# Time mixing with seven slots per head pair in place of eight, and a chain of 35 steps

## The chip, the core and the metric

The kernel runs on one core of a Trainium2 chip. The metric is the time of one execution in microseconds (us), measured on the device; lower is better. One program computes the whole trunk, and the change touches one stage of it.

## What is computed

A trunk of two layers over 256 tokens of width 2048, in float32, with 32 heads of 64. Every sub-layer has an RMS norm, a shift and scale and a gate that come from a condition vector `c` (adaLN). Layer A mixes over time with the recurrence below and ends in an MLP; layer B is chunked attention over a shared K/V, and another MLP. The change concerns the time mixing of layer A, cut here to what matters:

```python
xr, xw, xk, xv, xa, xg = [h + xx * mu[j] for j in range(6)]
r = xr @ w_r
k = xk @ w_k
v = xv @ w_v
...
def step(S, inp):
    r_t, w_t, k_t, v_t, kk_t, a_t = inp
    sa = jnp.einsum('bhvk,bhk->bhv', S, -kk_t)
    S = (S * w_t[:, :, None, :] + sa[..., None] * (kk_t * a_t)[:, :, None, :]
         + v_t[..., None] * k_t[:, :, None, :])
    y = jnp.einsum('bhvk,bhk->bhv', S, r_t)
    return S, y
...
y = ((y - mean) * lax.rsqrt(var + GN_EPS) * ln_w + ln_b)
y = y + jnp.sum(r_h * k_h * r_k, axis=-1, keepdims=True) * v_h
y = y * g
return y @ w_o
```

## The kernel before

Activations lie transposed, features on partitions. Weights come from HBM as float32 in tiles of 128 x 1024 (0.5 MB, tile `raw`, six buffers) and are split into a high and a low half: ScalarE casts `wH` (L378), VectorE subtracts to `wL` (L381), three buffers each. A projection (`proj2`) multiplies each 128-row block with `wH` against both halves of the activations (L412, 512 columns) and with `wL` against the high half (L413, 256 columns). Condition vectors of the later parts (adaLN) are summed on VectorE while other work runs: one `ada_step` reads one `raw` tile and adds it to `acc` (L454).

The 32 heads are 16 pairs, two heads on the 128 partitions, and time is cut into four chunks of 64 tokens. The class `Pair` writes a pair's whole work as a generator of 36 steps:

- **early**, steps 0 to 7: decay, normalized key, the factors `kr`, `bh`, `kh` (tiles `s`, L163 to L175, on VectorE), transposes of v.
- **invert**, steps 8 to 19. The recurrence within a chunk becomes the inverse of a triangular 64 x 64 matrix. Step 8 makes the products `gr` with `bh` and from them the masked `ar` (L212) and the pieces `da`, `co`; step 9 completes the start value `u`. Then five levels of two steps: the first transposes `u` to `tt` on VectorE (L239) and multiplies with the level's mask (`iv<-tt,al`, L111), ScalarE copies the product to `xs`; the second multiplies `iv<-u,xs` (L111), and VectorE adds it to `u` (L254). So levels 1 to 5 are steps 10/11, 12/13, 14/15, 16/17 and 18/19. Step 13 also makes the products `gr` with `kh` (L105) and the masked `mk` (L263). The last level works on the off-diagonal corner in a bank `ms`, and VectorE copies it into `uf` (L258).
- **late**, steps 20 to 35: for each of four chunks three steps with 64-wide products into the bank `lt` (L280 to L302), where the chunk's state goes on in `zs` (L307), then the group norm, the bonus and the gate. `py`, the result before the norm, lies in `lt`. ScalarE squares it in step 32, TensorE sums over heads in step 33, ScalarE takes the reciprocal root in step 34 and VectorE multiplies `py` with `ln_w` and that (L320), and step 35 makes the gate's product (L324) and applies it (L326).

`layer_a` lays the pairs out in slots. `SLOTS` is 8: pair j starts in slot 8(j+1), so that in a full slot four or five pairs are under way, each at another step: steps k, k+8, k+16, k+24 and so on share a slot (k is called the phase). In a slot the pairs' steps are issued first, those of the inversion first of all, then the late ones, then the early ones, each with the larger step first. They are pinned in this order on TensorE by `issue_after`; behind them come two of the 16 dense steps in which the next pair's k and r are projected (`proj_steps`, two row blocks each). The sum of the two halves of such a projection is taken on VectorE (L861, tiles `k` and `r`). On the other engines a scheduler fixes the order of instructions ahead of time, each engine running its own list strictly in order. From slot 16 on, three of four slots also take an adaLN step, 111 in all. After the last projection, from slot 128, the dense steps are 44 steps of the output projection `w_o` (`out_steps`), spread over the remaining 36 slots while the last pairs finish.

PSUM, the memory that matmuls write, has eight banks: `gr` and `iv` have one each, `ms`, `lt` and `pj` more. A bank is free again when its last reader is done.

Of the kernel before, what the change touches and what calls it, by code (L numbers as in the profile page):

```python
# [77 lines left out]
class Pair:  # L78

    EARLY, INVERT, LATE = 8, 12, 16  # L80
# [107 lines left out]
    def corner(self, l):  # L188
        t = self.b.psm() if l == 5 else self.b.pp.tile([P, 512], F32, tag="iv", bufs=1, name="iv")
        return t.rearrange("p (c t) -> p c t", t=H)[:, 0:4, :]  # L190

    def invert(self):
# [18 lines left out]
        ar = self.ar = s("ar", 3)  # L211
        nc.vector.tensor_tensor(out=ch(ar), in0=pg[:, :, C:P], in1=ui[:, :, C:P], op=ALU.mult)  # L212
# [24 lines left out]
        for l in range(1, 6):  # L237
# [13 lines left out]
            pi = self.corner(l)  # L251
            if l < 5:
                self.tiles(pi, xs, u, [(i, i) for i in range(4)])
                nc.vector.tensor_tensor(out=u, in0=u, in1=pi, op=ALU.add)  # L254
            else:
                self.tiles(pi, xs, u, up)
                for K in QS[::2]:
                    nc.vector.tensor_copy(uf[K, :, H:C], pi[K])  # L258
# [7 lines left out]
    def late(self):  # L266
# [45 lines left out]
        sq = self.square(py)  # L312
        yield
        var = b.psm()[:, :T]
        self.head_sums(var, sq)
        yield
        rg = s("sl", 1)
        nc.scalar.activation(rg, var, AF.Ln, scale=1.0 / C, bias=b.col(C_GN))
        nc.scalar.activation(rg, rg, AF.Exp, scale=-0.5)
        nc.vector.scalar_tensor_tensor(out=rg, in0=py, scalar=b.vec("ln_w", j), in1=rg, op0=ALU.mult, op1=ALU.mult)  # L320
        yield
        pg = b.psm()[:, :T]
        for i in range(2):
            mm(pg, lg[:, i, :], self.tg[:, i, :], start=(i == 0), stop=(i == 1))  # L324
        nc.vector.scalar_tensor_tensor(out=rg, in0=v, scalar=b.vec("ln_b", j), in1=rg, op0=ALU.add, op1=ALU.add)
# [4 lines left out]
class Body:  # L330
    RAW_BUFS = 6
    W_BUFS = 3
    SLOTS = 8
# [300 lines left out]
    def layer_a(self, st, sp):  # L634
# [198 lines left out]
        with ExitStack() as s1:  # L833
# [55 lines left out]
            for slot in range(S * NPAIR + Pair.STEPS):  # L889
# [13 lines left out]
                if slot < S * NPAIR:  # L903
                    if slot % S == 0:
                        dense = proj_steps(pairs[slot // S])
                    todo = 16 // S
                else:
                    if outs is None:
                        self.y_hl = self.new_hl()
                        outs = dense = out_steps()  # L910
                    todo = OUTS * (slot + 1 - S * NPAIR) // Pair.STEPS - n_out
                    n_out += todo
# [3 lines left out]
                if slot >= 2 * S and slot % 4 < 3:  # L916
                    self.ada()
# [314 lines left out]
```

## Time and profile before

| | before |
|---|---|
| median of 3 runs | 2668.64 us (2667.89 to 2671.07) |
| time of the profiled execution | 2668.82 us |
| span of its profile | 2667.0 us |
| mean granted TensorE clock | 0.992 |
| TensorE busy | 2594.2 us (97%) |
| VectorE busy | 2112.8 us (79%) |
| ScalarE busy | 1345.2 us (50%) |
| GpSimd busy | 208.7 us (8%) |
| stage of the pairs | about 196 to 711 us |

PE is TensorE's matmuls, PEld its weight loads, DVE VectorE, ACT ScalarE, POOL GpSimd, SP the engine that issues transfers. A row of a timeline has the start, the duration, the engine, the line, the operation, and the tile written and those read; what stands in brackets is the idle time ahead of it and what ended that. A group row has the total busy time, the mean duration in ns, and behind the second bar the idle time ahead of the group, with what ended most of it. A start plus the duration can lie behind the next start, since instructions of one engine overlap by a little; prices in the prediction go from start to start.

### The profile page before, as it was taken

How to read it: one execution, taken by the hardware profiler on the slowest of the kernel's cores; microseconds unless marked ns; L12 is line 12 of the kernel's file. 1: busy time of each engine (PE TensorE's matmuls, PEld its weight loads, DVE VectorE, ACT ScalarE, POOL GpSimd, SP SyncE). 2: the span in 40 equal slices, each digit the busy share in tenths (PEclk: the TensorE clock that was granted, in tenths of full speed). 3: DMA queues.
4: the chain of work that ended last, by engine and by line, in shares of the span. 5: the costliest groups of instructions: out<-in, count | busy, mean ns of one | idle time of the engine just before them, and what ended most of it. 6: DMA issues, size and time to landing. Idle time of an engine off the chain costs nothing.

```text
span 2667.0 us, 58173 instructions
## 1 busy us (share of the span) xinstructions
PE 2594.2 (97%) x23596; PEld 2229.2 (84%) x23596; DVE 2112.8 (79%) x3102; ACT 1345.2 (50%) x2435; POOL 208.7 (8%) x320
## 2 busy tenths in 40 slices
PE   7999999999999999999999999999999999999997
PEld 4787777887899888888888998877898888888886
DVE  6788888889789888888888898899887555555555
ACT  3346455555456445355365554565564463453554
POOL 0002223322110000000001100000100000000002
PEclk9999999999999999999999999999999999999998
DMA  9976556566778888889898679887766555555553
GB/s 349 312 244 211 185 179 207 180 214 199 246 236 312 309 317 327 319 324 332 318 329 293 238 242 331 318 274 256 265 218 235 190 189 184 188 189 186 186 189 119
DMA packets 207149, 662.62 MB, mean 248 GB/s; under 512 B 21408, under 2 KB 54560, under 8 KB 206880
## 3 DMA queue, kind: packets, MB, share of 16 engines
q1 hardware_dynamic: 204816, 656.36, 71.5%
q8 instruction: 185, 3.03, 0.5%
q10 hardware_dynamic: 2064, 2.54, 0.3%
q14 instruction: 84, 0.69, 0.1%
HBM read 656.72 MB, written 2.10 MB: 247 GB/s over the span
## 4 chain that ended last, share of the span: by engine, by line
PE 85%; DVE 5%; issue 4%; DMA 4%; ACT 2%; POOL 1%; DVEq 0%; SPq 0%; ACTq 0%; POOLq 0%
PE pj L412 45%; PE pj L413 23%; PE pj L402 2%; PE pj L401 2%; PE pj L403 2%; DMA raw<-w_ada 1%; DVE wL L381 1%; PE iv L111 1%; DVE acc L454 1%; PE gr L105 1%; ACT wH L378 1%; PE ms L115 1%; PE o L401 1%; PE ms L324 0%; PE ms L105 0%
## 5 line engine op out<-in xcount | busy, mean ns | idle before, releaser
L381 DVE TENSOR_TENSOR wL<-raw,wH 128x1024 fp32r<-128x1024 f32 x772 | 941.1, 1220 | 354.9 <-ACT wH L378 347.0
L378 ACT CAST wH<-raw 128x1024 fp32r<-128x1024 f32 x772 | 805.8, 1045 | 799.7 <-PE pj L412 650.0
L412 PE MATMUL pj<-aHL,wH 128*128 128x512 f32 x3328 | 1202.0, 403 | 1.9 <-DVE x L945 1.4
L413 PE MATMUL pj<-aHL,wL 128*128 128x256 f32 x3328 | 936.1, 281 | 0.4 <-DVE wL L381 0.4
L412 PEld LDWEIGHTS pj<-aHL,wH 128*128 128x128 f32 x3328 | 629.4, 189 | 154.4 <-issue 8.7
L412 PE MATMUL pj<-hHL,wH 128*128 128x512 f32 x2048 | 723.0, 398 | 0.0
L413 PEld LDWEIGHTS pj<-aHL,wL 128*128 128x128 f32 x3328 | 629.4, 189 | 3.1 <-issue 0.8
L413 PE MATMUL pj<-hHL,wL 128*128 128x256 f32 x2048 | 574.4, 281 | 0.0
L412 PEld LDWEIGHTS pj<-hHL,wH 128*128 128x128 f32 x2048 | 384.6, 188 | 94.4 <-DVE hHL L991 0.2
L413 PEld LDWEIGHTS pj<-hHL,wL 128*128 128x128 f32 x2048 | 386.8, 189 | 0.1
L454 DVE SCALAR_TENSOR_TENSOR acc<-rada,ct,acc 128x1024 f32<-128x1024 f32 x256 | 327.2, 1278 | 8.5 <-DMA rada<-w_ada 7.6
L518 POOL TENSOR_TENSOR ss<-ss,sq 128x256 f32<-128x256 f32 x56 | 52.6, 940 | 1590.8 <-ACT sq L517 1590.5
L1016 DVE SCALAR_TENSOR_TENSOR x<-pj,mod,x 128x256 f32<-128x256 f32 x256 | 123.4, 482 | 58.6 <-PE pj L413 54.9
L454 DVE SCALAR_TENSOR_TENSOR acc<-raw,ct,acc 128x1024 f32<-128x1024 f32 x104 | 136.2, 1309 | 15.3 <-DMA raw<-w_ada 14.9
L988 ACT ACTIVATE t<-t 128x256 f32<-128x256 f32 x112 | 46.8, 418 | 123.5 <-DVE t L960 123.5
L401 PE MATMUL pj<-aHL,wH 128*128 128x258 f32 x384 | 109.0, 284 | 0.0
L402 PE MATMUL pj<-aHL,wH 128*128 128x258 f32 x384 | 108.9, 284 | 0.0
L403 PE MATMUL pj<-aHL,wL 128*128 128x258 f32 x384 | 108.0, 281 | 0.0
L403 PEld LDWEIGHTS pj<-aHL,wL 128*128 128x128 f32 x384 | 73.2, 191 | 0.2
L402 PEld LDWEIGHTS pj<-aHL,wH 128*128 128x128 f32 x384 | 72.6, 189 | 0.1
L401 PEld LDWEIGHTS pj<-aHL,wH 128*128 128x128 f32 x384 | 72.2, 188 | 0.2
L990 ACT ACTIVATE t<-t 128x256 f32<-128x256 f32 x128 | 53.4, 417 | 3.4
(249 smaller groups left out, 2815.5 us busy)
## 6 DMA issues: line engine op xcount, KB each, us to landing
raw<-w_up SPq DMA_DIRECT2D x256, 512.0 KB, 4.2
raw<-w_down SPq DMA_DIRECT2D x256, 512.0 KB, 4.3
rada<-w_ada SPq DMA_DIRECT2D x209, 512.0 KB, 5.8
raw<-w_ada SPq DMA_DIRECT2D x111, 512.0 KB, 4.3
rada<-w_ada_kv SPq DMA_DIRECT2D x64, 512.0 KB, 6.1
rawa<-w_ada SPq DMA_DIRECT2D x32, 512.0 KB, 6.9
rawa<-w_ada_t SPq DMA_DIRECT2D x32, 512.0 KB, 7.5
raw<-w_k SPq DMA_DIRECT2D x32, 512.0 KB, 4.0
```

The costliest lines, as they stand in the source:

```text
L378: nc.scalar.copy(Hf, raw)
L381: eng.tensor_tensor(out=Lf, in0=raw, in1=Hf, op=ALU.subtract)
L401: nc.tensor.matmul(ps, H[:, i, :], a(kt)[:, 0, :], start=(first and kt == 0), stop=False)
L402: nc.tensor.matmul(ps, H[:, i, :], a(kt)[:, 1, :], start=False, stop=False)
L403: ins = nc.tensor.matmul(ps, L[:, i, :], a(kt)[:, 0, :], start=False, stop=(last and kt == KT - 1))
L412: nc.tensor.matmul(ps, H[:, i, :], a(kt), start=(kt == 0), stop=False)
L413: ins = nc.tensor.matmul(ps[:, 0, :], L[:, i, :], a(kt)[:, 0, :], start=False, stop=(kt == KT - 1))
L454: nc.vector.scalar_tensor_tensor(out=self.acc, in0=raw, scalar=ck, in1=self.acc, op0=ALU.mult, op1=ALU.add)
L518: (eng or nc.gpsimd).tensor_tensor(out=self.ss, in0=self.ss, in1=sq, op=ALU.add)
L988: nc.scalar.activation(t, t, AF.Relu)
L990: nc.scalar.activation(t, t, AF.Square)
L1016: nc.vector.scalar_tensor_tensor(out=x, in0=ps[:, i, :], scalar=self.mods[(layer, 5)][:, n:n + 1], in1=x, op0=ALU.mult, op1=ALU.add)
```

## The change

`SLOTS` becomes 7 and the late part one step shorter, so that a pair has 35 steps, five times seven: in a full slot five pairs are under way, at steps k, k+7, k+14, k+21 and k+28. The rest makes this fit:

- The 16 dense steps of a pair are spread over seven slots: 2, 2, 2, 3, 2, 2, 3. The whole stage has 147 slots instead of 164, and the output projection's 44 steps are spread over 35 slots. An adaLN step stands in five of six slots, again 111 in all.
- Steps 10 and 17 now share a slot, and both would write the one bank `iv`; step 17 takes a bank of `ms`.
- `ar` is masked in step 11 instead of step 8, from the bank `gr`, which stays occupied until then.
- At the end of the chain `py` is read earlier: step 32 also copies `py` times `ln_w` into SBUF on ScalarE (16 new instructions in all), step 33 takes the logarithm right behind the sum over heads, step 34 the exponential, and VectorE multiplies the two tiles in SBUF there (a `tensor_tensor` in place of the `scalar_tensor_tensor` that read `py` in PSUM); the gate's product stands in the same step.

No matmul and no VectorE instruction is added or taken away: 18,392 instructions on TensorE and 3,072 on VectorE as listed in both programs.

```diff
@@ class Pair
-    EARLY, INVERT, LATE = 8, 12, 16
+    EARLY, INVERT, LATE = 8, 12, 15
...
-    def corner(self, l):
-        t = self.b.psm() if l == 5 else self.b.pp.tile([P, 512], F32, tag="iv", bufs=1, name="iv")
+    def corner(self, l, second=False):
+        t = self.b.psm() if l + second >= 5 else self.b.pp.tile([P, 512], F32, tag="iv", bufs=1, name="iv")
...
         self.each(lambda c: pg[:, c, :], lambda c: ch(bh)[:, c, :], lambda c: kr[:, c, :])
-        ar = self.ar = s("ar", 3)
-        nc.vector.tensor_tensor(out=ch(ar), in0=pg[:, :, C:P], in1=ui[:, :, C:P], op=ALU.mult)
...
-            pi = self.corner(l)
+            pi = self.corner(l, True)
             if l < 5:
                 self.tiles(pi, xs, u, [(i, i) for i in range(4)])
                 nc.vector.tensor_tensor(out=u, in0=u, in1=pi, op=ALU.add)
+                if l == 1:
+                    ar = self.ar = s("ar", 3)
+                    nc.vector.tensor_tensor(out=ch(ar), in0=pg[:, :, C:P], in1=ui[:, :, C:P], op=ALU.mult)
...
         sq = self.square(py)
+        rg = s("sl", 1)
+        nc.scalar.activation(rg, py, AF.Copy, scale=b.vec("ln_w", j))
         yield
         var = b.psm()[:, :T]
         self.head_sums(var, sq)
-        yield
-        rg = s("sl", 1)
-        nc.scalar.activation(rg, var, AF.Ln, scale=1.0 / C, bias=b.col(C_GN))
-        nc.scalar.activation(rg, rg, AF.Exp, scale=-0.5)
-        nc.vector.scalar_tensor_tensor(out=rg, in0=py, scalar=b.vec("ln_w", j), in1=rg, op0=ALU.mult, op1=ALU.mult)
+        rs = s()
+        nc.scalar.activation(rs, var, AF.Ln, scale=1.0 / C, bias=b.col(C_GN))
         yield
         pg = b.psm()[:, :T]
         for i in range(2):
             mm(pg, lg[:, i, :], self.tg[:, i, :], start=(i == 0), stop=(i == 1))
+        nc.scalar.activation(rs, rs, AF.Exp, scale=-0.5)
+        nc.vector.tensor_tensor(out=rg, in0=rg, in1=rs, op=ALU.mult)
         nc.vector.scalar_tensor_tensor(out=rg, in0=v, scalar=b.vec("ln_b", j), in1=rg, op0=ALU.add, op1=ALU.add)
         nc.vector.tensor_tensor(out=v, in0=pg, in1=rg, op=ALU.mult)
         yield
@@ class Body
-    SLOTS = 8
+    SLOTS = 7
...
-                    if slot % S == 0:
+                    k = slot % S
+                    if k == 0:
                         dense = proj_steps(pairs[slot // S])
-                    todo = 16 // S
+                    todo = 16 * (k + 1) // S - 16 * k // S
...
-                if slot >= 2 * S and slot % 4 < 3:
+                if slot >= 2 * S and slot % 6 < 5:
                     self.ada()
```

Two places show how the order moves. The first is the start of one slot on TensorE. Before, in phase 3 of eight, steps 19 and 11 of two inversions (`ms<-u,xs`, `iv<-u,xs`), the gate's product of step 35 and step 27 stand between two runs of projections:

```order
L413 MATMUL pj<-aHL,wL 128x256
L111 MATMUL ms<-u,xs 32x32 x8
L111 MATMUL iv<-u,xs 32x32 x16
L324 MATMUL ms<-tg,lg 128x256 x2
L287 MATMUL lt<-g,uf_2147 64x64 x2
L412 MATMUL pj<-aHL,wH 128x512
```

After, in phase 3 of seven, steps 17 and 10 and the late steps 31 and 24 do:

```order
L415 MATMUL pj<-aHL,wL 128x256
L111 MATMUL ms<-u,xs 32x32 x16
L111 MATMUL iv<-tt,al 32x32 x16
L292 MATMUL lt<-mk,vp 64x64 x2
L295 MATMUL lt<-kr,zs 64x64 x2
L297 MATMUL lt<-ar,sa 64x64 x2
L288 MATMUL lt<-g,uf_2148 64x64 x2
L414 MATMUL pj<-aHL,wH 128x512
```

There is more chain work between two runs of projections, and the runs are longer in two of seven slots.

The second is VectorE around step 11's sum (into `u`) and step 12's transpose (to `tt`). The other names are the early steps' tiles of a younger pair (`s`, `kr`, `bh`, `kh`), the weight halves, the projected `k`, and the output `v` of the oldest pair. Before:

```order
L258 COPY uf_0_2147<-ms_7134 32x4x32 x2
L254 TENSOR_TENSOR u_6947<-u_6947,iv_7145 128x128
L326 TENSOR_TENSOR v_86<-ms_7163,sl_7103 128x256
L239 STREAM_TRANSPOSE tt_7194<-u_6947 128x128
L163 SCALAR_TENSOR_TENSOR s_7173<-s_7173,s_7172 128x256
L167 SCALAR_TENSOR_TENSOR s_7178<-s_7178,k_6676 128x256
L164 SCALAR_TENSOR_TENSOR s_7171<-s_7173,s_7171 128x256
L175 TENSOR_TENSOR kh_7181<-s_7178,s_7119 128x256
L166 SCALAR_TENSOR_TENSOR s_7235<-k_6676,vecs_66,s_7171 128x256
L174 SCALAR_TENSOR_TENSOR s_7309<-r_6906,vecs_66,s_7178 128x256
L381 TENSOR_TENSOR wL_7241<-raw_7238,wH_7240 128x1024
L861 TENSOR_TENSOR k_7191<-pj_6983,k_7191 128x256
```

After (lines of the changed file; L252 is the sum, L237 the transpose, L259 the copies to `uf`, L456 the adaLN sum, L308 the state):

```order
L166 SCALAR_TENSOR_TENSOR s_7194<-k_6596,vecs_66,s_7093 128x256
L172 TENSOR_TENSOR kr_7251<-r_6820,e01_0_2145 128x4x64
L170 TENSOR_TENSOR kr_7251<-s_7194,e01_0_2145 128x4x64
L171 TENSOR_TENSOR bh_7102<-bh_7102,s_7194 128x256
L175 TENSOR_TENSOR kh_7103<-s_7100,s_7030 128x256
L456 SCALAR_TENSOR_TENSOR acc_6526<-raw_7488,ct_68,acc_6526 128x1024
L863 TENSOR_TENSOR k_7113<-pj_6886,k_7113 128x256
L383 TENSOR_TENSOR wL_7119<-raw_7116,wH_7118 128x1024
L252 TENSOR_TENSOR u_6928<-u_6928,iv_7156 128x128
L308 SCALAR_TENSOR_TENSOR zs_7190<-zs_6955,pc_5449,lt_6791 128x64
L259 COPY uf_0_2147<-ms_7208 32x4x32 x2
L237 STREAM_TRANSPOSE tt_7219<-u_6928 128x128
```

The sum and the transpose have moved from ahead of the early operations to behind them, and behind a subtraction `wL` and, here, an adaLN sum.

## Prediction

> **What bounds the kernel now.** I read the page first: busy shares, then the chain that ended last.
>
> ```profile
> PE 2594.2 (97%) x23596; PEld 2229.2 (84%) x23596; DVE 2112.8 (79%) x3102; ACT 1345.2 (50%) x2435; POOL 208.7 (8%) x320
> PE 85%; DVE 5%; issue 4%; DMA 4%; ACT 2%; POOL 1%; DVEq 0%; SPq 0%; ACTq 0%; POOLq 0%
> ```
>
> TensorE is busy 97% of the span and carries 85% of the chain. A change that leaves every matmul in place can gain only where TensorE waits, or where the order of the matmuls makes them cost less. The change acts in the stage of the head pairs, so next come the busy times in its three parts: filling, steady, emptying (busy us and instruction counts of PE, PEld, DVE, ACT, POOL, then granted clock, DMA share, GB/s).
>
> ```profile
> 196.00:343.00 147.00, 135.07 (x2235) 112.53 (x2237) 125.31 (x222) 76.53 (x192) 35.83 (x47) 0.97 0.62 200
> 343.00:628.00 285.00, 279.51 (x5830) 228.69 (x5828) 247.40 (x471) 155.03 (x441) 79.73 (x110) 1.00 0.59 188
> 628.00:711.00 83.00, 78.21 (x1556) 67.48 (x1557) 70.28 (x120) 35.26 (x101) 13.72 (x21) 1.00 0.70 231
> ```
>
> The stage is 515 us long. TensorE idles 11.9 us while it fills, 5.5 us in the steady part and 4.8 us while it empties. VectorE is 87% busy in the steady part, ScalarE 54%. So the most that waits can give back is 22 us, and VectorE is the engine that can take TensorE's place. The chain of waits gives the steady period: one product of the step that opens each inversion, one pair later.
>
> ```profile
> 504.70 1.02 PE gr L105 x16
> 532.89 1.02 PE gr L105 x16
> ```
>
> That is 28.19 us per pair, so 3.52 us per slot with eight slots, and with seven slots about 4.0 us for the same work.
>
> **The change part by part.** *Fewer switches of tile size.* Chain products use 32- or 64-wide tiles of the array, projections 128-wide. TensorE's timeline (start, duration):
>
> ```profile
> 501.41 0.45 PE L111 MATMUL iv<-tt,al 32*32 32x32 f32 x32
> 501.79 0.33 PE L291 MATMUL lt<-mk,vp 64*64 64x64 f32 x4
> 501.96 0.28 PE L294 MATMUL lt<-kr,zs 64*64 64x64 f32 x4
> 502.07 0.28 PE L296 MATMUL lt<-ar,sa 64*64 64x64 f32 x4
> ...
> 502.42 0.28 PE L280 MATMUL lt<-vp,mk 64*64 64x64 f32 x4
> 502.64 0.50 PE L412 MATMUL pj<-aHL,wH 128*128 128x512 f32 x1
> 502.98 0.28 PE L413 MATMUL pj<-aHL,wL 128*128 128x256 f32 x1
> 503.09 0.40 PE L412 MATMUL pj<-aHL,wH 128*128 128x512 f32 x1
> 503.33 0.28 PE L413 MATMUL pj<-aHL,wL 128*128 128x256 f32 x1
> ...
> 504.04 0.28 PE L413 MATMUL pj<-aHL,wL 128*128 128x256 f32 x1
> 504.25 0.45 PE L111 MATMUL iv<-u,xs 32*32 32x32 f32 x32
> ```
>
> From start to start: the first 64-wide group takes 0.17 us, the next 0.11 (switch 0.06); leaving 64-wide for the projection takes 0.22 instead of 0.11 (0.11); the first L412 takes 0.34, the next 0.24 (0.10); from the last L413 to the 32-wide group 0.21 instead of 0.11 (0.10). One round of three switches so shows 0.37 us, 0.12 each; if the group that is left hides part of its own switch, as the 0.38 us of the 32-wide group lets one suspect, up to 0.18 each. Fewer slots mean fewer rounds: counting tile sizes along the order of both programs I get 455 switches in the stage before and 408 after, 47 fewer. Term 1: 47 × 0.15 = −7.0 us (−5.6 at 0.12, −8.5 at 0.18). It falls on TensorE itself, so nothing hides it.
>
> *More work per slot.* Each step now has about 4.0 us instead of 3.5 for its answer to come back from VectorE or ScalarE, so the waits of the steady part should mostly go. I take −4.0 of the 5.5 us (0 to −5.5). But a new wait comes. Before, the sum of step 11 and the transpose of step 12 stand next to each other on VectorE, ahead of the early steps' operations. After, the two stand behind those (second place on VectorE shown above). Durations for pricing them, VectorE's timeline:
>
> ```profile
> 525.90 0.58 DVE L258 COPY uf<-ms 32x128 f32<-32x128 f32 x2 [0.48 <-PE ms L111]
> 526.51 0.29 DVE L254 TENSOR_TENSOR u<-u,iv 128x128 f32<-128x128 f32 x1
> 526.86 0.43 DVE L163 SCALAR_TENSOR_TENSOR s<-s 128x256 f32<-128x256 f32 x1
> 527.20 0.30 DVE L239 STREAM_TRANSPOSE tt<-u 128x128 f32<-128x128 f32 x1
> ...
> 530.61 0.41 DVE L861 TENSOR_TENSOR k<-pj,k 128x256 f32<-128x256 f32 x1
> 530.95 0.27 DVE L307 SCALAR_TENSOR_TENSOR zs<-zs,pc,lt 128x64 f32<-128x64 f32 x1
> 531.14 1.39 DVE L381 TENSOR_TENSOR wL<-raw,wH 128x1024 fp32r<-128x1024 f32 x1
> ```
>
> Start to start, a 128x256 operation takes 0.34 us, a sum L254 0.35 (0.2 behind another pair's), zs 0.2, the uf copies 0.6. In the shown place after, from the older pair's sum at the start of phase 3 to the transpose (L237) that step 12 needs, VectorE has this sum and a transpose (0.6), s and s (0.7), ar (0.3), five early operations (1.7), k (0.34), wL (1.1), the sum and zs (0.4), uf and the transpose itself (0.9): 6.0 us. Of TensorE's work, the rest of phases 3 and 4 stands beside it: priced group by group from such rows, phase 3 takes 3.5 us and phase 4 3.0; less 0.4 for the group that releases the first sum, 6.1 us. That is just hidden. In that place an adaLN step (acc) stands in it too, and costs what this group row says:
>
> ```profile
> L454 DVE SCALAR_TENSOR_TENSOR acc<-raw,ct,acc 128x1024 f32<-128x1024 f32 x104 | 136.2, 1309 | 15.3 <-DMA raw<-w_ada 14.9
> ```
>
> About 1.2 us from start to start, so TensorE waits 6.0 + 1.2 − 6.1 = 1.1 us. The inversion's group stands first in its slot, and everything else on TensorE is queued behind it, the projections too. By the order, an acc falls there in 7 of the 16 pairs: +7.7 us (0 to 1.1 × 16 = 17.6). Term 2: 7.7 − 4.0 = +3.7 us.
>
> *The filling.* Its worst place before, on VectorE:
>
> ```profile
> 274.11 0.28 DVE L254 TENSOR_TENSOR u<-u,iv 128x128 f32<-128x128 f32 x1
> 274.31 0.68 DVE L263 TENSOR_TENSOR mk<-gr,csts 128x512 f32<-128x512 f32 x1
> ...
> 275.57 1.21 DVE L381 TENSOR_TENSOR wL<-raw,wH 128x1024 fp32r<-128x1024 f32 x1
> ...
> 277.80 0.30 DVE L239 STREAM_TRANSPOSE tt<-u 128x128 f32<-128x128 f32 x1
> ```
>
> On TensorE this is one wait, and the clock falls behind it (the last three columns of the two stretches are granted clock, DMA share, GB/s):
>
> ```profile
> 278.24 0.65 PE L111 MATMUL iv<-tt,al 32*32 32x32 f32 x32 [4.15 <-DVE tt L239]
> 278.00:282.00 4.00, 3.76 (x68) 3.41 (x69) 3.13 (x4) 0.64 (x2) 0.61 (x1) 0.50 0.66 202
> 282.00:286.00 4.00, 4.00 (x52) 3.14 (x51) 1.07 (x4) 0.21 (x1) 0.00 (x0) 0.65 0.57 185
> ```
>
> 4.15 us are waited, then 4 us run at 0.50 and 4 at 0.65, worth 2.0 + 1.4 = 3.4 us: 7.5 together. The Trainium skill, "TensorE: Matmul & The Clock Gate", section "HAM oscillation — how this bites in real kernels", says that idle gaps of over about 3.4 us throttle the array again; the trace agrees, with 4.15 us ahead of the granted 0.50. By that rule the waits of 1.1 us added above cost no clock. In the changed order the operations between this sum and its transpose are spread over two slots, and I find no second place like it. Term 3: −5.0 us (0 if another queue forms, as VectorE is 85% busy here; −7.5 if all goes).
>
> *The emptying.* At the end of the projections five pairs are under way instead of four and a half: 105 steps are left, in 35 slots, instead of 100 in 36. The 44 steps of the output projection are spread over them either way. The matmuls of the five steps are moved here, not added. There is more cover per slot, but the later steps press closer on VectorE (85% busy here). Term 4: +1.0 us (−2 to +4).
>
> *Edits with one answer: nothing.* The loads on SP's queue stay in number and size; the 111 adaLN loads stand in five of six slots instead of three of four, and VectorE's waits for them, 14.9 us over 104 steps in the row above, stay as they are. ar moves to a later step, and is read only in the late steps, nine steps on. Step 17 takes an ms bank, since steps 10 and 17 now share a slot; by the order each bank is free a slot earlier. The new copy of py on ScalarE, 16 times, is of a quarter of the cast's size,
>
> ```profile
> L378 ACT CAST wH<-raw 128x1024 fp32r<-128x1024 f32 x768 | 804.2, 1048 | 798.5 <-PE pj L412 650.0 <-issue 37.4 <-PE pj L402 35.6
> ```
>
> so under 16 × 1.05 = 17 us on an engine that idles 130 us in the steady part alone; if that cover failed, 17 us would be the price. The gate's product now has both inputs in SBUF. The nearest rows for that: L254 above with one input in PSUM, 0.29 us, and the same shape with both in SBUF,
>
> ```profile
> L227 DVE TENSOR_TENSOR u<-u,csts 128x128 f32<-128x128 f32 x16 | 18.6, 1161 | 6.3 <-POOL u L221 5.3
> ```
>
> 1.16 us: 0.87 more. I take 0, since it stands in the slot with the most TensorE work (about 5.5 us), and carry 16 × 0.87 = 14 us as a rival. The Trainium skill, "SBUF — State Buffer", section "Who interferes with whom", says that a VectorE instruction with two SBUF inputs contends with a GpSimd instruction that reads SBUF; the slow L227 agrees with it, and the rule speaks against this edit.
>
> **Sum.** −7.0 + 3.7 − 5.0 + 1.0 = −7.3 us against the profiled execution's 2668.8 us: 2661.5. That execution lies 0.2 us above the median of 2668.6, so nothing is corrected. A measurement of this kernel can tell about 0.2%, 5.3 us, from no change.
>
> **The rivals.** *A: the forecast*, 2661.5.
>
> *B: the new wait does not come.* The acc's step is issued at the end of a slot, and if VectorE runs ahead of TensorE there, its 1.2 us lie in a gap; the 37.6 us in which VectorE idles in the steady part speak for it, the order against it. Then −7.3 − 7.7 = −15: 2653.8.
>
> *C: the wait comes in every pair.* The place is then late by the acc or by as much of something else; 17.6 instead of 7.7 us: +2.6, 2671.4, no change that can be told. VectorE's slack of 0.1 us in the pairs without acc speaks for it.
>
> *D: VectorE becomes the bound there, and it is slower.* wL stands in that queue, and its cast on ScalarE waits for the projection to free a buffer: 650 us of such waits over the whole trace in the cast's row. If the cast comes late by its own 1.05 us in every pair, VectorE stands still in order, and the wait is 1.1 + 1.05 in 7 pairs and 1.05 − 0.1 in 9: 23.6 us instead of 7.7, so −7.3 + 15.9 = +8.6: 2677.4. It decides from (15.0 + 5.3) / 16 = 1.3 us per pair. Against it: 3.6 us of other work (4.8 with an acc) stand ahead of wL in that place, and phase 3 as a whole is 3.5 us long.
>
> *E: the two-input product lies on the path.* All 14 us of it: +6.7, 2675.5. Against it speaks the cover named.
>
> That the change doesn't do what it says is excluded by the order: only this stage is moved, with the same matmuls.
>
> **How the numbers follow.** A 0.36, B 0.14, C 0.26, D 0.19, E 0.05. Faster by over 0.2% is A and B: 0.50; within it C: 0.26; slower D and E: 0.24. The range leaves out the far ends of B and D: below, B with terms 1 and 3 at their ends, −15 − 1.5 − 2.5 = −19, gives 2650; above, D with the fall of the clock (3.4 us) once where such a wait adds up, 2680.8, gives 2680. A's own range is 2655 to 2668.
>
> **What would show it.** Right: a steady period of 27.5 to 28 us between the opening products, about 408 switches, no wait over 3.4 us in the filling and a granted clock near 1.00 there, and waits of about 1 us of iv for tt (L237) once in some pairs, none in others. Wrong: a steady period over 28.2 us; waits for tt in every pair (C), with wL's wait for the cast ahead of them (D); L326 near 1.2 us and TensorE waiting for the products behind it (E); a new wait above 3.4 us with a clock of 0.5 behind it.

## Result, and the profile after

| | before | after |
|---|---|---|
| median of 11 runs each | 2669.12 us (2666.75 to 2671.07) | 2675.70 us (2668.90 to 2678.07) |
| profiled execution, its span | 2668.82, 2667.0 us | 2675.70, 2673.9 us |

The ratio is 1.0019, 95% interval 1.0011 to 1.0028: slower by about 5 us (6.6 by the medians), where 7 us faster was forecast. The time lies inside the range that was given, on the other side of no change. A second series of the same kernel gave 1.0022 (1.0010 to 1.0033).

First the three parts of the pairs' stage again: filling, steady, emptying (busy us and counts of PE, PEld, DVE, ACT, POOL, then granted clock, DMA share, GB/s):

```profile
196.00:343.00 147.00, 136.49 (x2258) 114.75 (x2260) 132.92 (x231) 81.83 (x206) 38.31 (x51) 0.98 0.67 212
343.00:627.00 284.00, 272.30 (x5699) 224.33 (x5696) 241.24 (x459) 153.48 (x435) 77.11 (x107) 0.99 0.58 180
627.00:719.00 92.00, 83.86 (x1666) 72.34 (x1664) 72.13 (x123) 37.01 (x110) 16.24 (x21) 0.94 0.64 210
```

TensorE idles 10.5, 11.7 and 8.1 us, where it was 11.9, 5.5 and 4.8. The steady part is as long as before, the emptying 9 us longer, at a mean clock of 0.94. The steady period shows in the chain:

```profile
475.06 1.02 PE gr L105 x16
...
504.20 1.02 PE gr L105 x16
...
531.33 1.02 PE gr L105 x16
```

One pair takes 29.1 us, the next 27.1. In the slow one stands the place that the prediction named: step 12's transpose comes too late from VectorE (a wait of 1.66 us). Here it is in a later pair, from step 17's sum (L252 into `u` from `ms`) to the transpose (VectorE, then TensorE, then the clock in the third last column of two stretches):

```profile
578.02 0.27 DVE L252 TENSOR_TENSOR u<-u,ms 128x128 f32<-128x128 f32 x1
579.21 0.43 DVE L163 SCALAR_TENSOR_TENSOR s<-s 128x256 f32<-128x256 f32 x1 [0.91 <-ACT s L157]
...
582.14 1.64 DVE L456 SCALAR_TENSOR_TENSOR acc<-raw,ct,acc 128x1024 f32<-128x1024 f32 x1
583.71 0.41 DVE L863 TENSOR_TENSOR k<-pj,k 128x256 f32<-128x256 f32 x1
584.04 1.30 DVE L383 TENSOR_TENSOR wL<-raw,wH 128x1024 fp32r<-128x1024 f32 x1
585.26 0.27 DVE L252 TENSOR_TENSOR u<-u,iv 128x128 f32<-128x128 f32 x1
585.46 0.27 DVE L308 SCALAR_TENSOR_TENSOR zs<-zs,pc,lt 128x64 f32<-128x64 f32 x1
585.65 0.57 DVE L259 COPY uf<-ms 32x128 f32<-32x128 f32 x2
586.25 0.31 DVE L237 STREAM_TRANSPOSE tt<-u 128x128 f32<-128x128 f32 x1
```

```profile
586.71 0.45 PE L111 MATMUL iv<-tt,al 32*32 32x32 f32 x32 [2.41 <-DVE tt L237]
```

```profile
584.00:588.00 4.00, 1.59 (x58) 1.13 (x54) 3.96 (x9) 0.88 (x3) 0.25 (x1) 1.00 0.61 167
588.00:592.00 4.00, 4.00 (x57) 3.19 (x54) 3.18 (x5) 1.86 (x4) 0.00 (x0) 0.59 0.83 261
```

VectorE waits 0.91 us for ScalarE's `s`, then works without a gap and in its order; acc, k and wL stand ahead of step 11's sum. TensorE waits 2.41 us and, from 588.7 us on, runs 3.41 us at half clock. Such waits over the steady part, before and after:

```profile
PE iv L111 <- DVE tt L239: 1.3, 2, 0.7
PE iv L111 <- DVE tt L237: 9.6, 7, 2.6
```

In the emptying TensorE stops within one group of 32 products, with nothing to wait for:

```profile
659.49 0.38 PE L111 MATMUL iv<-tt,al 32*32 32x32 f32 x21
664.14 0.42 PE L111 MATMUL iv<-tt,al 32*32 32x32 f32 x11 [4.27 <-issue]
```

and the clock falls there too (10 us each; before, no stretch of the emptying is under 1.00):

```profile
657.00:667.00 10.00, 5.73 (x136) 5.13 (x136) 6.57 (x10) 3.26 (x9) 1.75 (x5) 0.84 0.79 273
667.00:677.00 10.00, 10.00 (x218) 8.33 (x221) 6.88 (x16) 2.86 (x8) 0.00 (x0) 0.82 0.35 108
```

The instruction queue (q8) brings 16 KB packets, 185 in all for 47,192 matmuls and weight loads, one for about 128 matmuls with their loads. The last packet before the end of this stop began at 661.6 us, when TensorE had already stood for 1.7 us.

**Ledger of the stage**, worked out from each trace: from the first product of step 0 (214.4 us before) to the last gate's product (710.6). "Waits" is the sum of TensorE's gaps, "clock" half the time for which the clock record shows 0.50, "work" the rest, so TensorE's work at full clock. "Emptying" is the stage's length from the first product of the output projection on. The two profiles of the changed kernel differ by 4.0 us in the stage, so smaller differences of single profiles say little; the ratios are from the timed runs against the kernel before.

| kernel | ratio (95%) | stage us | waits | clock | work | emptying |
|---|---|---|---|---|---|---|
| before | 1 | 496.2 | 21.1 | 5.1 | 470.0 | 80.8 |
| after | 1.0019 (1.0011 to 1.0028) | 504.3 | 29.0 | 11.9 | 463.3 | 91.8 |
| again (= after) | 1.0022 (1.0010 to 1.0033) | 500.3 | 25.5 | 11.9 | 462.8 | 89.5 |
| chain35_8 | 1.0007 (0.9997 to 1.0016) | 496.8 | 23.7 | 3.4 | 469.7 | 81.1 |
| acc_short_8 | 0.9963 (0.9949 to 0.9977) | 484.1 | 14.1 | 0.0 | 469.9 | 81.0 |
| acc_short_7 | 0.9997 (0.9982 to 1.0011) | 499.4 | 24.7 | 11.9 | 462.8 | 86.8 |
| pin | 1.0086 (1.0073 to 1.0099) | 520.7 | 38.9 | 18.8 | 463.1 | 90.9 |
| pin2 | 1.0010 (1.0000 to 1.0020) | 502.8 | 22.9 | 17.1 | 462.8 | 91.4 |
| flip2 | 1.0018 (1.0008 to 1.0028) | 499.7 | 25.3 | 10.2 | 464.2 | 88.6 |
| ada_half | 1.0244 (1.0229 to 1.0259) | 491.0 | 21.2 | 8.5 | 461.2 | 84.2 |
| tail_short | 1.0017 (1.0007 to 1.0026) | 500.1 | 26.3 | 10.2 | 463.6 | 84.2 |
| tail_light | 0.9981 (0.9971 to 0.9991) | 493.0 | 20.3 | 10.2 | 462.4 | 79.5 |
| pin2_light | 0.9963 (0.9950 to 0.9977) | 492.1 | 20.6 | 8.5 | 462.9 | 79.3 |
| pin5 | 1.0060 (1.0047 to 1.0072) | 493.3 | 22.1 | 6.8 | 464.4 | 81.0 |
| pin6 | 0.9989 (0.9980 to 0.9997) | 496.0 | 22.3 | 10.2 | 463.5 | 84.4 |
| early_ada | 0.9978 (0.9969 to 0.9987) | 491.4 | 21.8 | 6.8 | 462.7 | 79.3 |
| late_8 | 0.9993 (0.9983 to 1.0003) | 493.5 | 19.7 | 4.6 | 469.1 | 84.9 |
| early_8 | 0.9961 (0.9948 to 0.9974) | 487.7 | 16.9 | 0.0 | 470.7 | 74.5 |
| early_8_again | 0.9975 (0.9966 to 0.9985) | 488.3 | 17.6 | 0.0 | 470.7 | 74.9 |
| early_7 | 0.9999 (0.9991 to 1.0008) | 504.5 | 29.5 | 13.7 | 461.3 | 77.4 |

### The profile page after: what moved, and what is told of

It reads as the page before. It is cut to its first block, busy times and chain, and to the rows that moved or that the text cites. A ratio compares the mean times of both kernels' runs of the same rounds, so it can differ in the third digit from the quotient of the medians.

```text
span 2673.9 us, 58156 instructions
## 1 busy us (share of the span) xinstructions
PE 2591.8 (97%) x23596; PEld 2231.0 (83%) x23596; DVE 2116.0 (79%) x3102; ACT 1350.2 (50%) x2451; POOL 211.7 (8%) x320
## 4 chain that ended last, share of the span: by engine, by line
PE 84%; DVE 7%; issue 4%; DMA 3%; ACT 2%; POOL 0%; DVEq 0%; ACTq 0%; POOLq 0%; SPq 0%
PE pj L414 44%; PE pj L415 22%; DVE wL L383 2%; PE pj L404 2%; PE pj L403 2%; PE pj L405 2%; DVE acc L456 1%; DMA raw<-w_ada 1%; PE iv L111 1%; PE gr L105 1%; PE ms L115 1%; DMA rada<-w_ada 1%; PE ms L324 1%; PE ms L105 1%; PE m L692 0%
## 5 line engine op out<-in xcount | busy, mean ns | idle before, releaser
L456 DVE SCALAR_TENSOR_TENSOR acc<-rada,ct,acc 128x1024 f32<-128x1024 f32 x256 | 327.6, 1280 | 9.5 <-DMA rada<-w_ada 8.9
L456 DVE SCALAR_TENSOR_TENSOR acc<-raw,ct,acc 128x1024 f32<-128x1024 f32 x104 | 135.4, 1302 | 7.3 <-DMA raw<-w_ada 6.9
```

The lines of the kernel that those rows point to most:

```text
L456: nc.vector.scalar_tensor_tensor(out=self.acc, in0=raw, scalar=ck, in1=self.acc, op0=ALU.mult, op1=ALU.add)
```

## Experiments

The expectations weigh these theories. **Q**: step 11's sum and step 12's transpose stand too late in VectorE's queue, and half clock follows such waits. **L**: the other edits, with longer work at the end of the chain, cost the time. **F**: VectorE is too full with five pairs under way, in any order. **P**: the loss is an accident of instruction loading. **I**: in the emptying, TensorE's instruction fetches stand behind bursts of adaLN transfers. **D** (not the prediction's rival D): the adaLN sums hold up the chain there. Phase 5 is the slot of step 12.

**1. Are the other edits to blame?** chain35_8 is the changed kernel with

```diff
-    SLOTS = 7
+    SLOTS = 8
-                if slot >= 2 * S and slot % 6 < 5:
+                if slot >= 2 * S and slot % 4 < 3:
```

> All other edits of the change (chain of 35 steps, gate's product and reciprocal root moved, ar in step 11, step 17 in another bank), but eight slots per pair and the adaLN step in three of four slots, as before. Theory Q: these edits are free, 2665 to 2670. Theory L: 2672 or more. Theory F: 2665 to 2670.

1.0007: no difference that can be told, and theory L falls. The loss belongs to the seven slots.

**2. How much of it is the adaLN sum in the queue?** acc_short_7 and acc_short_8 add only the first 64 of 1024 columns in the stage and leave the rest out:

```diff
+            n = 64 if self.short else HK * P
-            nc.vector.scalar_tensor_tensor(out=self.acc, in0=raw, ...
+            nc.vector.scalar_tensor_tensor(out=self.acc[:, :n], in0=raw[:, :n], ...
```

> The changed kernel, but in the pairs' stage each adaLN sum adds only the first 64 of its 1024 columns, so most of these sums are left out; transfers, order and counts stay. One acc then takes about 0.15 instead of 1.3 us. Theory Q: the four steady places with an acc ahead of step 11's sum wait about 1.1 us less each, like the pairs without one, and the clock does not fall there (1.7 us each): 2662 to 2668. Theory L: 2672 to 2676. Theory F: also faster, as VectorE loses some 3 us of work per pair, 2660 to 2668, but then with waits gone in all phases alike, not in the one place.

> The kernel before with the same shortening of the adaLN sums (the first 64 of 1024 columns are added in the pairs' stage, the rest is left out), as the control. Theory Q: before, step 11's sum and its transpose do not stand behind an acc, so in the steady part little is won: 2664 to 2668, all of it in the filling and emptying. Theory F: 2660 to 2664. With both shortened, theory Q lets the seven slots come out 3 to 8 us ahead of the eight, by the fewer switches of tile size.

Eight slots gained 10 us, seven about 6 us against the change. Seven slots came out 10.6 us behind (2670.4 and 2659.8), where theory Q put them ahead; no theory had 2670.4, and 2659.8 lies just under F's figure. In the profiles, 9 of the 12 us that the eight slots' stage gained are waits and half clock of the filling. The seven slots' steady part gained nothing: 10.9 us of waits and 10.2 of half clock, after 11.7 and 3.4 in the change. With the sums short, the place still waits, up to 2.3 us:

```profile
489.40 0.28 DVE L459 SCALAR_TENSOR_TENSOR acc<-raw,ct,acc 128x64 f32<-128x64 f32 x1 [2.07 <-DMA raw<-w_ada]
...
492.55 0.41 DVE L171 TENSOR_TENSOR bh<-bh,s 128x256 f32<-128x256 f32 x1
492.88 0.41 DVE L175 TENSOR_TENSOR kh<-s 128x256 f32<-128x256 f32 x1
493.22 0.63 DVE L459 SCALAR_TENSOR_TENSOR acc<-raw,ct,acc 128x64 f32<-128x64 f32 x1
493.77 1.65 DVE L383 TENSOR_TENSOR wL<-raw,wH 128x1024 fp32r<-128x1024 f32 x1
...
586.16 0.24 DVE L459 SCALAR_TENSOR_TENSOR acc<-raw,ct,acc 128x64 f32<-128x64 f32 x1
```

```profile
493.11 0.66 POOL L207 TENSOR_TENSOR s<-bh,pc 128x256 f32<-128x256 f32 x1 [1.10 <-DVE bh L171]
493.73 0.61 POOL L207 TENSOR_TENSOR s<-kh,pc 128x256 f32<-128x256 f32 x1
```

bh and kh release two GpSimd operations, and VectorE's next two take 0.63 instead of 0.24 and 1.65 instead of 1.2 us beside them. The short sums removed less from the queue than was expected. And a sum, however short, stands in VectorE's queue until its transfer has landed: here 2.07 us, just ahead of step 17's sum, and 26.2 us over the steady part, where the change has 5.0. So these runs don't isolate the queue. Nor did the waits go in all phases alike, as theory F had it: the amount of VectorE's work alone doesn't explain them.

**3. Taking the place apart.** pin issues each transpose behind its sum (`flip`) and holds the younger pair's early operations, the projections' and the adaLN step's VectorE work behind step 12's transpose. pin2 also moves step 10's transpose to the end of step 9. flip2 has the transposes of pin2 and no pinning.

```diff
                 nc.vector.tensor_tensor(out=u, in0=u, in1=pi, op=ALU.add)
+                tt_ = flip()
...
-                    with tc.issue_after(last):
-                        next(pr.gen)
+                    with tc.issue_after(last):
+                        if pin is not None and -at < Pair.EARLY:
+                            with tc.issue_after(pin):
+                                next(pr.gen)
+                        else:
+                            next(pr.gen)
+                    if -at == Pair.EARLY + 3:
+                        pin = pr.turned
```

> Seven slots as in the change, but on VectorE the transpose for step 12 stands directly behind step 11's sum, and the younger pair's early operations and the slot's subtractions and adaLN sums stand behind both. Theory Q (the changed kernel loses to the queue on VectorE in phase 5, and to the slow clock that such waits bring): the waits of iv for tt in that phase fall from 11.5 us in the steady part to under 4, the clock falls at most once in the steady part, and the time is 2660 to 2666 us, below the kernel before. Theory L (the other edits, the longer work per step on ScalarE and VectorE at the end of the chain, cost the time): 2673 to 2677, as the change. Theory F (VectorE is simply too full with five pairs under way, whatever the order): the wait goes to another step, 2672 to 2678.

> Seven slots with step 12's transpose pinned behind step 11's sum, ahead of the younger pair's early operations, as in the run named pin, but step 10's transpose is taken out of the way too: it stands at the end of step 9, so that it no longer waits behind step 17's sum (1.05 us in every pair there). Theory Q: these waits go, those of phase 5 stay gone, the half clock with them: 2656 to 2664. Theory F (VectorE too full with five pairs): 2670 to 2690, with the waits in another place.

> The changed kernel with every transpose of the inversion issued directly behind the sum that it needs (step 10's at the end of step 9), and nothing pinned: step 11's sum still stands behind the early operations, k and wL, but the transpose no longer behind zs and the uf copies, which saves 0.6 us of the queue where uf stood in it (the four steady pairs with an acc). Theory Q: those waits fall from 2.3 to about 1.7 us, some of the falls of the clock go: 2668 to 2672. Theory F: 2672 to 2677.

> The changed kernel once more, unaltered, to see which of its waits come again in another execution. Theory Q (queue on VectorE ahead of step 11's sum and step 12's transpose, and the half clock behind such waits): the same four steady pairs with an acc in that place wait 1.6 to 2.7 us again, 2671 to 2677. Theory P (the loss is an accident of instruction loading, the 4.3 us stop in the middle of a group of matmuls at 664 us): without such a stop the time is 2666 to 2670.

pin was 23 us slower than the kernel before, which no theory had. The waits of iv that tt ended fell to 2.8 us in the steady part, as theory Q asked, but step 10's transpose now stood behind step 17's sum of the same slot, 1.05 us in every pair, as here (the releaser named had long been done):

```profile
505.99 0.45 PE L111 MATMUL iv<-tt,al 32*32 32x32 f32 x32 [1.05 <-POOL uf L254]
```

pin2 took that away, and of the waits of iv for tt in the steady part one was left, of 3.46 us behind an adaLN transfer. But filling and steady part together took 411.4 us, as in the two profiles of the change (412.5 and 410.8; the 375 us of a later expectation are counted from 250 us on): TensorE's column sums of acc now waited for VectorE (1.1 and 1.7 us), and half clock cost 8.5 us in the two parts. 2671.5 against 2673.8 of the unaltered kernel on the same chip: the wait was turned into others, and theory Q's 2656 to 2664 was missed. flip2 moved nothing (2673.8, in theory F's range). In the second profile of the change, the same four places waited again (2.36, 1.64, 2.20, 2.41 us) and the stop came at the same matmul, 2.63 us this time, so it is no accident of one execution, as theory P had it.

**4. The emptying.** tail_short cuts the adaLN sums there to 64 columns, tail_light the transfers as well (and clears acc in place of a first sum); pin2_light is pin2 with the latter.

```diff
+            self.nc.sync.dma_start(out=t[:, :64], in_=src[:, :64])
```

> The changed kernel, but the adaLN sums issued in the 35 slots behind the last projection add only 64 of 1024 columns (most of these 29 sums is left out; their transfers stay). Theory D (in the emptying, VectorE's adaLN sums hold up the chain): the emptying falls from 90-92 us to about 82, idle time and half clock of TensorE there (13 us together) fall below 6. Theory I (TensorE runs out of instructions there, since its fetches stand behind the bursts of weight transfers): the stops in the middle of a group, 3 to 5 us with the half clock behind them, stay, 88 to 91 us.

> As the run before, and the transfers of these adaLN tiles are cut to 64 columns as well (about 15 MB less to move in the emptying; most of these sums and loads is left out). Theory I: the stops in the middle of a group and the half clock behind them go, the emptying takes 80 to 83 us, 2662 to 2667 us in all. Theory D: no different from the run with short sums and full transfers. If instructions run out because the chain's small matmuls use them up faster than they can be fetched, whatever else moves, the stops stay in both.

> The run pin2 with the adaLN sums and transfers issued in the emptying cut to 64 of 1024 columns (most of these sums is left out). If the queue and the instruction stops add up: 2671.5 - 11 = 2660 or below, with the emptying at 80 us and the steady part as in pin2, 375 us. If the stops come for another reason, the emptying stays near 90 us.

With short sums alone the profiled emptying fell to 84.2 us, with three stops of 0.8 to 1.2 us at packet boundaries and no half clock, nearer to theory D than to I; but the median stayed (2671.7). With the transfers cut no stop and no half clock was left:

```profile
628.00:707.00 79.00, 77.76 (x1661) 67.54 (x1660) 47.17 (x115) 37.03 (x110) 10.55 (x21) 1.00 0.34 105
```

2660.8. Between these two profiles 5 us of the difference lie in the emptying and 6 behind the stage. By the medians the transfers are the larger part of what is lost (11 us), and the sums alone bring about 1 us by the ratios, which can't be told from nothing; by the profiles of the emptying the two are about even. pin2_light, 2658.6, shows that the gain adds to pin2's.

**5. The adaLN steps laid otherwise, with all work in place.** ada_half has one in every second slot, pin5 one in every slot up to the last projection and one in two behind it (115 in all), with pin2's pins. early_ada is the changed kernel with

```diff
-                if slot >= 2 * S and slot % 6 < 5:
+                if slot > 2 * S and (slot < S * NPAIR or slot % 5 in (0, 2)):
```

again 111 steps, 14 instead of 29 of them in the emptying; pin6 adds pin2's pins.

> The changed kernel with an adaLN step in every second slot instead of five of six: 67 instead of 111 in the pairs' stage, the other 44 run later beside the MLPs. No acc stands ahead of step 11's sum any more but in one pair. Theory Q: the pairs' stage gains the excess of those places, 4 to 8 us, and the later stages lose little, as VectorE is 55% busy there: 2664 to 2670. Theory F: VectorE loses 44 x 1.3 = 57 us of work in the stage, waits go in all phases: 2655 to 2662. If the later stages are bound by transfers, what is won is lost there.

> The run pin2 (transposes out of the way, step 12's pinned behind step 11's sum ahead of the early operations) with the adaLN steps laid otherwise: one in every slot up to the last projection and one in every second slot behind it, so fewer of them in the emptying (17 instead of 29). No adaLN sum stands between step 17's transpose and step 11's sum but rarely. Theory Q with theory I: the steady part's waits of iv for tt stay gone, the emptying loses part of its stops: 2660 to 2667 us, ahead of the kernel before. Theory F (VectorE too full): 2670 or more, since the steady part gets 1.3 us more VectorE work per pair.

> The changed kernel with the same 111 adaLN steps laid earlier: one in every slot up to the last projection, 14 instead of 29 in the emptying; nothing else. By the order, an acc stands ahead of step 11's sum in one steady pair instead of four. Theory I (fetches behind bursts of adaLN transfers stop TensorE in the emptying): the emptying falls from about 90 to 81 to 84 us. Theory Q: the steady part loses the 2.3 us waits and two or three falls of the clock, 4 to 7 us. Together 2660 to 2666. Theory F (VectorE too full in the steady part): the steady part grows by 3 us or more and the total stays at 2668 to 2674.

> The run before, with the transposes directly behind their sums and step 11's pinned ahead of the early operations, as in pin2. Theories I and Q: 2658 to 2666, not slower than the run before. If pinning only turns one wait into another, as it did in pin2, it is 2 us or more slower than the run before.

ada_half lost 64 us: its stage is 491 us, but behind it the adaLN sums are not ready and TensorE waits 14.9 and 20.8 us for them. pin5's stage is short (493 us), but the rest takes about 14 us longer: TensorE waits there for 21 us, mostly for VectorE, instead of 7 in the second profile of the change. What delays VectorE was not settled. early_ada, 2661.6, beats the kernel before by 7 us, as theories I and Q together had it. But its steady part has 12.2 us of waits and 3.4 of half clock, no less than the change (11.7 and 3.4), and the gain lies in the emptying (1.4 us instead of 13.2): that is theory I's part alone. Pinning (pin6, 2664.3) adds nothing.

**6. Does that belong to seven slots?** early_8 and late_8 are the kernel before with all adaLN steps ahead of the emptying, or with 36 of them in it; early_7 is the changed kernel with all ahead (`0 < slot < S * NPAIR`).

```diff
-                if slot >= 2 * S and slot % 4 < 3:
+                if 2 * S < slot < S * NPAIR:
```

> The kernel before (eight slots) with its 111 adaLN steps one in every slot up to the last projection, none in the emptying. If the stops for instructions belong to the seven slots' emptying, there is little to win here (0.5 us of stops before): 2665 to 2670, and seven slots with early adaLN stay ahead by the 7 us of fewer switches. If early adaLN is good for any schedule, 2658 to 2663, level with the seven slots.

> The kernel before with more adaLN steps in the emptying: one in each of its 36 slots (27 before), two of three slots ahead of it, again 111. Theory I: transfers in the emptying stop TensorE's instruction fetches, so the emptying grows from 81 to 84 to 90 us with stops in the middle of groups and the half clock behind them, 2669 to 2677. If the stops need the seven slots' denser chain, the emptying stays at 81 to 82 us and the time at 2664 to 2669.

> Seven slots with all 111 adaLN steps laid ahead of the emptying, one in each slot up to the last projection, none behind it; the level counterpart of early_8. Theory I alone (the loss of seven slots lay in the emptying): 7 us of fewer switches come through, 2650 to 2654, ahead of early_8. Theory Q (the queue ahead of step 12's transpose and the half clock behind it eat the switches' gain in the steady part): 2657 to 2663, level with early_8 or behind it, with waits of iv for tt of over 8 us in the steady part.

> The kernel before with its adaLN steps laid ahead of the emptying, once more on the same chip as the run beside it: 2656 to 2661 by all theories.

It does not: early_8, 0.9961, is the fastest kernel with all work in place, 12 us under the kernel before on its chip and 6 us in its second series. Its emptying has nothing left to wait for (profile of the second series):

```profile
628.00:703.00 75.00, 74.83 (x1469) 64.60 (x1467) 39.78 (x89) 34.04 (x97) 11.20 (x21) 1.00 0.23 71
```

But the emptying is not the whole of it: against the kernel before, waits and half clock fall by 5 us in the emptying and by 7 in the filling, and the steady part waits 2 to 3 us longer.

On the same chip early_7 took 2670.3 and early_8 2663.4; no theory had early_7 so slow. That comparison is not level. early_7 starts its sums sooner, and its filling has 23.5 us of waits and half clock, early_8's 8.7; one wait of 6.1 us is among them. But early_7's steady part also has 6.8 us of half clock, and early_8's none. late_8's emptying grew to 84.9 us, in theory I's range, but with one stop of 0.55 us alone, and its time can't be told from that of the kernel before (0.9993). So with eight slots more transfers in the emptying did not bring the stops. Stops at packet boundaries came with eight slots as well (2.5 us once, in acc_short_8's emptying), and half clock in the emptying only at late_8's end (1.2 us lost).

## Why the prediction failed

- **Term 1, fewer switches: right.** −7.0 forecast, 470.0 to 463.3 us of work measured, −6.7, and 461 to 464 in every run with seven slots. The traces count 455 and 408 switches, as forecast, and with all the other edits but eight slots (chain35_8) it is 455 switches and 469.7 us.
- **Term 2, waits in the steady part: the failing step.** The place was right, and so was TensorE's side of it where an acc stands in it: 6.1 us of work set, 6.2 to 6.6 measured. The price of VectorE's queue was not right. From step 17's sum to the end of step 12's transpose I set 6.0 + 1.2 = 7.2 us with an acc, as if VectorE never stood still there; it took 7.7 to 9.0. Idle time in the queue, which I had put at nothing, is up to 1.8 us of that: 0.91 us for ScalarE's `s` in the place shown, and 1.24 us for an adaLN transfer ahead of the longest wait (first line below). The other part is acc beside GpSimd's operations (the lines behind it): in three of the four it took 1.6 us from start to start, as in the place shown (582.14 to 583.71), instead of the 1.2 set.

```profile
408.68 1.29 DVE L456 SCALAR_TENSOR_TENSOR acc<-raw,ct,acc 128x1024 f32<-128x1024 f32 x1 [1.24 <-DMA raw<-w_ada]
```

```profile
582.04 0.66 POOL L207 TENSOR_TENSOR s<-bh,pc 128x256 f32<-128x256 f32 x1 [2.26 <-DVE bh L171]
582.66 1.59 POOL L207 TENSOR_TENSOR s<-kh,pc 128x256 f32<-128x256 f32 x1
```

An acc stood there in four of the eleven pairs from 315 us on, and these waited 1.7 to 2.6 us instead of 1.1 (one of them at 324 us, still in the filling). In the other seven the queue took 5.2 to 6.8 us (6.0 set) and TensorE's work beside it 4.4 to 6.8, and four of them waited 0.3 to 1.1 us instead of none. All waits of the steady part grew by 6.2 us instead of 3.7, and two falls of the clock there, 3.4 us, were not in the term at all. Together +9.6 us.

- **The price of a wait.** I took waits under 3.4 us to cost no clock, by the rule in the Trainium skill's "TensorE: Matmul & The Clock Gate", section "HAM oscillation — how this bites in real kernels", and the fall behind 4.15 us. The traces differ, the one before the change already (granted clock in the third last column):

```profile
238.75 0.45 PE L111 MATMUL iv<-tt,al 32*32 32x32 f32 x32 [2.36 <-DVE tt L239]
240.40:243.80 3.40, 3.40 (x43) 2.61 (x41) 2.38 (x6) 1.34 (x4) 1.52 (x3) 0.50 0.77 189
```

After the change, waits of 1.68, 2.36, 2.62 and 2.41 us were each followed by 3.41 us at half clock, 1.7 us lost each; waits of 2.52 and 1.66 us were not. Where the wait lies decides: in every profile, all changes of the granted clock lie whole multiples of 3.413 us apart, to within 0.01 us. Cut into pieces on that grid, the twenty profiles (from 100 us on) have 69 pieces at full clock in which TensorE idled 1.9 us or more, and all 69 were followed by a piece at half clock; so were 31 of 51 with 1.5 to 1.9 us, and 14 of 14,711 with less. The border of two pieces cut the wait of 2.52 us into 1.83 and 0.69.

- **Term 3, the filling:** the named place went, but waits of 2.5, 1.7 and 2.4 us came. Waits and clock together fell by 3.1, not 5.0 us.
- **Term 4, the emptying: the second failing step.** +1.0 forecast, with +4 as the end; waits grew by 3.3 us and half clock by 5.1, +8.4. That TensorE could stop with nothing to wait for, its instructions coming late, was in no rival. That the adaLN transfers delay them fits tail_light, early_ada and early_8; late_8 speaks against it, and pin has a stop of 1.73 us with the transfers 20% busy. So this cause is argued, not shown.
- **Sum:** −6.7 + 9.6 − 3.1 + 8.4 = +8.2 us in the stage, 1.4 us won behind it: the 6.9 us between the two profiled executions.
- **Rivals.** The slower result came by neither D nor E, to which it was given. E is out: the product with both inputs in SBUF (L326) takes 0.447 us on average, not 1.16, so the rule on two SBUF inputs did not bite there, though it (the Trainium skill's "SBUF — State Buffer", "Who interferes with whom") fits acc and wL beside GpSimd in experiment 2.

```profile
L326 DVE TENSOR_TENSOR sl<-sl,s 128x256 f32<-128x256 f32 x16 | 7.1, 447 | 4.2 <-ACT s L325 4.2
```

C came nearest in the steady part: waits of 0.3 to 2.6 us in eight of eleven pairs. In the place shown VectorE stood still for ScalarE's `s`, and not for a cast, as D had it.

What is shown: fewer slots save 7 us of TensorE's work, and TensorE's waits and half clock cost 15 and 11 us more than before in the two profiles of the change, mostly in the steady part's one place on VectorE and in the emptying. That VectorE's queue there is late is read from the traces; no run took it away without bringing other waits. What stays open: whether an order exists in which seven slots come out ahead of eight with the adaLN steps laid as freely (the orders that were pinned only moved the wait), why instructions come late in the emptying, and why early_8's filling gained.

## What to carry to other kernels

In a pipeline of long chains, fewer and fuller slots save the switches between kinds of work, but every engine with a fixed order must get each chain's answer out within one slot: list what stands in its queue between two steps of the same chain, and price it with its neighbours' interference and with the answers that the queue itself stands still for. A wait of TensorE of about 2 us or more should be priced with the 1.7 us of half clock that may follow. Where side work can be laid freely, try its place before rebuilding the pipeline: here moving all of it ahead of the emptying won 12 and 6 us with eight slots in two series, where the change had been forecast to win 7. It is a thing to try and not a rule: laying more of it into the emptying (late_8) cost nothing that could be told.

## What the hardware showed

- Half clock comes in pieces of 3.41 us (or two and three of them) on one grid of 3.413 us per profile. A piece with 1.9 us or more of TensorE's idle time was always followed by one at half clock (69 of 69), one with under 1.5 us hardly ever (14 of 14,711); one wait or several close together count alike (three of 0.3 to 0.6 us from 640 to 643 us after the change). Kernels with seven slots lost 7 to 19 us to it in the stage, with eight 0 to 5.
- TensorE's instructions come in packets of 16 KB. Of 49 stops of 0.5 us or more with nothing to wait for in the stage (twenty profiles), 47 ended 2.2 to 2.7 us after such a packet began. The longest, 4.27 us, came with the transfers 79% busy in its stretch; with the adaLN transfers cut there was none in the emptying.
- Beside a GpSimd operation (over 0.3 us of it) VectorE's wL of 128x1024 took 1.42 us on average in the stage after the change (23 of them), without one 1.22 (44); acc 1.38 (29) and 1.23 (73).
